# Sparse attention with both key groups in one iteration and zero-padded operands, in a two-block model on one core

## Chip, core and metric

The kernel runs on one core of one Trainium2 chip. The metric is the device time of one execution in microseconds; the median of three runs before the change is 2191.86 us (2190.61 to 2194.94). A profile of one execution gives the instructions of each engine: PE (TensorE), DVE (VectorE), ACT (ScalarE), POOL (GpSimd) and the DMA queues. The program itself is put in order at build time: every engine gets a fixed list of instructions, and semaphores make one engine wait for another.

## What is computed

256 tokens of width 1024 pass through a first block (a mixer of three branches, then a mixture of experts with 16,384 small experts) and a second block (feed-forward layers, a convolution mixer, differential attention). The change lies in two branches of the mixer.

The **stick-breaking branch** has 8 heads of 64: scores z, then weights exp(log sigmoid(z) + the sum of log sigmoid(-z) over the keys between), times the values. In short:

```python
log_1m = where(before, log_sigmoid(-z), 0.0)
after = cumsum(log_1m, reverse=True) - log_1m
a = where(before, exp(log_sigmoid(z) + after), 0.0); out = a @ v
```

The **sparse branch** (NSA) has 8 heads of 64 in two groups; the four heads of a group share keys and values. A query attends in three ways, each with its own softmax and its own gate: to 15 compressed keys (each made of 32 neighbouring tokens by a product with a [2048, 64] matrix), to selected blocks of 64 keys, and to a window. At 256 tokens there are four blocks and four are selected, and the window is 256 long, so these two read all earlier keys:

```python
s = q @ k.T * scale - slope * dist
p = softmax(where(valid, s, -1e30)); o = g0*p_c@v_c + g1*p_s@v_s + g2*p_w@v_w
```

## The kernel before, in words

All weights come as a stream of units [128, 1024] of float32. `Stream.next` (L252) issues a unit's DMA on SP's queue, ScalarE makes a rounded copy `whi` (L268) and VectorE the rest `wlo` (L269). `proj_T` (L75) multiplies a unit by the 256 tokens with three matmuls per tile of 128 rows (`mm3`, L68 to L73): 24 records of 256 columns a unit. Four raw and three finished units can be held at a time.

`mixer` (from L1056) is the phase of the change. `proj2` makes two such projections into one PSUM bank (tag pp, two banks) and evacuates it. The other banks are five of tag bk for everything between and one of tag ob for a branch's output. The phase runs HGRN2 (a linear recurrence, L1115 to L1219), stick breaking (L1221 to L1263), NSA (L1266 to L1381), then 24 units of projections for the merge gates (L1384 to L1386), the gated sum of the three branches (L1396 on) and the output projection. The order on each engine is not that of the text: at build time a scheduler that works with estimated costs takes, for each engine, the earliest instruction of the text that is ready. So where an attention chain waits for another engine, TensorE's list has projection matmuls of later steps (pp) in between.

**Stick breaking**, one head at a time (L1238). Two heads lie in one tile of 128 rows, so that a head's queries and keys are 64 rows. A head's scores of 256 + 128 columns (L1245, L1246), its causal mask added by a bfloat16 product with the identity (L1247, L1248), three exponential-type steps of ScalarE over 384 columns (L1250 to L1252), one step of VectorE, products with a triangle for the running sums (L1254 to L1256), one more exponential (L1258), and the product with the values, 64 output rows (L1260, L1261).

**Compression** (L1286 to L1310). `xa` holds for each of the 32 places of a block the tokens of 16 blocks for both groups, 64 rows a group, zero where row and column belong to different groups. For keys and then for values 32 matmuls run over it, with 64 columns standing and 64 moving (L1303).

**Attention of NSA** (L1329 to L1381): for four pairs p, two groups gg and two tiles of queries qt, 16 iterations:

```python
q = nq[ks, p, qt * 128 : qt * 128 + 128]              # 64 rows
mm(sc[...], q, nk[ks, a, :kl], start=True, stop=False)  # a = 0, 1
mm(sc[...], ident_b, bias[:, h, 256 - kl :], start=False, stop=True)
mm(sc2[:, :16], q, kcT[ks, :], start=True, stop=False)
```

with kl 128 or 256. Maxima (L1346, L1347), exponentials with sums (L1352, L1354), reciprocal, gates and scaling (L1356 to L1360), transposes by TensorE (L1363, L1367), copies out of PSUM (L1371, L1372), products with the values (L1378) and with the compressed values (L1380). The output of a pair goes through `put` (L1106 to L1108). A float32 matmul appears as two records in the trace, a transpose or a bfloat16 matmul as one.

## Time and profile before

| what | value |
|---|---|
| median of the runs | 2191.86 us |
| span of the profiled execution | 2191.6 us |
| TensorE busy | 99% of the span |
| VectorE, ScalarE, POOL busy | 68%, 53%, 1% |
| granted TensorE clock, mean | 0.997 |
| read from memory | 367.38 MB |

The span runs from the first to the last instruction of the profiled execution; that execution's time beyond the span is not in the profile, and the median of the other runs stands 0.3 us above it. A busy time of TensorE adds up modelled ends of matmuls that overlap; the distance from one start to the next is in the timeline.

### The profile page before, as it was taken

The numbers are of one execution on the slowest core, as the hardware profiler recorded it, in microseconds if no ns is written. First come the engines' busy times: TensorE is split into PE (matmuls) and PEld (weight loads), VectorE is DVE, ScalarE is ACT, GpSimd is POOL, SyncE is SP. The second block draws the span as 40 slices with busy tenths as digits, with TensorE's granted clock in tenths as the row PEclk, the third lists the DMA queues.
The fourth block names the chain that finished last, engine by engine and source line by source line (L and its number), as shares of the span: only waits on it lengthen the run. The fifth ranks groups of instructions, "written<-read, shape, count | busy, mean of one in ns | idle before, by whom it ended". The sixth has DMA issues, their size and how long they took to land.

```text
span 2191.6 us, 37898 instructions
## 1 busy us (share of the span) xinstructions
PE 2161.8 (99%) x14823; PEld 1979.5 (90%) x14823; DVE 1480.1 (68%) x2705; ACT 1152.1 (53%) x2088; POOL 26.7 (1%) x27
## 2 busy tenths in 40 slices
PE   8999999999999999999999999999999999999998
PEld 7978898999999998888888999999999999878998
DVE  5865658799888895556557655776557555677554
ACT  5544354554577775554446544545446444466443
POOL 0000000000000000000000000000000000100000
PEclk9999999999999999999999999999999999999999
DMA  7334245555544445656555755556655654534652
GB/s 232 104 110 126 78 143 176 164 183 184 183 136 135 135 135 184 193 195 213 195 193 174 253 187 183 188 168 209 192 183 174 209 185 154 183 106 144 203 183 97
DMA packets 103010, 370.89 MB, mean 169 GB/s; under 512 B 12208, under 2 KB 12976, under 8 KB 102704
## 3 DMA queue, kind: packets, MB, share of 16 engines
q1 hardware_dynamic: 102688, 367.69, 52.1%
q8 instruction: 117, 1.92, 0.4%
q0 software_dynamic: 144, 0.79, 0.1%
q14 instruction: 61, 0.50, 0.1%
HBM read 367.38 MB, written 1.05 MB: 168 GB/s over the span
## 4 chain that ended last, share of the span: by engine, by line
PE 93%; DVE 3%; ACT 1%; issue 1%; DMA 0%; SPq 0%; DVEq 0%; ACTq 0%
PE gu L72 9%; PE gu L73 9%; PE gu L71 9%; PE hp L71 6%; PE hp L72 6%; PE hp L73 6%; PE pacc L72 5%; PE pacc L71 5%; PE pacc L73 5%; PE acc L72 5%; PE acc L71 5%; PE acc L73 5%; PE pp L71 3%; PE pp L73 3%; PE pp L72 3%; PE gp L885 3%
## 5 line engine op out<-in xcount | busy, mean ns | idle before, releaser
L268 ACT ACTIVATE whi<-raw 128x1024 fp32r<-128x1024 f32 x670 | 704.0, 1058 | 791.0 <-PE gu L72 214.5
L269 DVE TENSOR_TENSOR wlo<-raw,whi 128x1024 fp32r<-128x1024 f32 x670 | 819.4, 1225 | 355.9 <-ACT whi L268 352.9
L71 PE MATMUL gu<-hT,whi 128*128 128x256 f32 x1568 | 444.7, 284 | 0.4 <-ACT sg L438 0.4
L73 PE MATMUL gu<-hT,wlo 128*128 128x256 f32 x1568 | 444.3, 283 | 0.3 <-DVE wlo L269 0.3
L72 PE MATMUL gu<-hT,whi 128*128 128x256 f32 x1568 | 444.3, 283 | 0.0
L71 PEld LDWEIGHTS gu<-hT,whi 128*128 128x128 f32 x1568 | 300.1, 191 | 3.5 <-ACT sg L438 0.6
L72 PEld LDWEIGHTS gu<-hT,whi 128*128 128x128 f32 x1568 | 300.4, 192 | 2.7
L73 PEld LDWEIGHTS gu<-hT,wlo 128*128 128x128 f32 x1568 | 300.4, 192 | 0.5 <-DVE wlo L269 0.5
L71 PE MATMUL hp<-hT,whi 128*128 128x256 f32 x1024 | 294.8, 288 | 1.0 <-ACT Ga L850 1.0
L73 PE MATMUL hp<-hT,wlo 128*128 128x256 f32 x1024 | 289.7, 283 | 0.0
L72 PE MATMUL hp<-hT,whi 128*128 128x256 f32 x1024 | 289.6, 283 | 0.0
L71 PEld LDWEIGHTS hp<-hT,whi 128*128 128x128 f32 x1024 | 196.2, 192 | 1.4 <-ACT Ga L850 1.2
L72 PEld LDWEIGHTS hp<-hT,whi 128*128 128x128 f32 x1024 | 196.3, 192 | 0.2
L71 PE MATMUL pacc<-whi,pa 128*128 128x512 f32 x504 | 196.1, 389 | 0.0
L72 PE MATMUL pacc<-wlo,pa 128*128 128x512 f32 x504 | 196.1, 389 | 0.0
L73 PEld LDWEIGHTS hp<-hT,wlo 128*128 128x128 f32 x1024 | 196.1, 191 | 0.0
L73 PE MATMUL pacc<-whi,pa 128*128 128x512 f32 x504 | 196.1, 389 | 0.0
L72 PE MATMUL acc<-wlo,a 128*128 128x512 f32 x352 | 138.9, 395 | 0.0
L73 PE MATMUL acc<-whi,a 128*128 128x512 f32 x352 | 138.2, 393 | 0.0
L71 PE MATMUL acc<-whi,a 128*128 128x512 f32 x352 | 136.8, 391 | 0.0
L452 DVE TENSOR_TENSOR sg<-gu,rbc 128x256 f32<-128x256 f32 x80 | 33.9, 423 | 132.3 <-PE gu L73 132.3
L73 PE MATMUL pp<-hT,wlo 128*128 128x256 f32 x416 | 119.7, 288 | 0.0
(431 smaller groups left out, 3555.0 us busy)
## 6 DMA issues: line engine op xcount, KB each, us to landing
raw<-w_peer_dram SPq DMA_DIRECT2D x264, 512.0 KB, 3.4
raw<-w_ffn_dram SPq DMA_DIRECT2D x264, 512.0 KB, 4.1
raw<-w_mix_dram SPq DMA_DIRECT2D x83, 512.0 KB, 3.7
raw<-w_conv_dram SPq DMA_DIRECT2D x32, 512.0 KB, 4.3
raw<-w_qo_dram SPq DMA_DIRECT2D x16, 512.0 KB, 4.0
g<-g_norm_dram SPq DMA_DIRECT2D x12, 512.0 KB, 3.8
raw<-w_k_dram SPq DMA_DIRECT2D x8, 512.0 KB, 3.4
raw<-w_v_dram SPq DMA_DIRECT2D x8, 512.0 KB, 4.7
```

The costliest lines, as they stand in the source:

```text
L71: mm(out, l[0], r[0], start=start, stop=False)
L72: mm(out, l[0], r[1], start=False, stop=False)
L73: self.last_mm = mm(out, l[1], r[0], start=False, stop=stop)
L268: c.nc.scalar.activation(hi, raw, AF.Copy)
L269: c.last_lo = c.nc.vector.tensor_tensor(lo, raw, hi, op=ALU.subtract)
L452: V.tensor_tensor(sg, gu[:, 0, :], c.rbc, op=ALU.mult)
L885: nc.tensor.matmul(gp[:, m, :], r, cg, start=True, stop=True)
```

## The change

- Stick breaking: `sbq` has a second copy of each pair's space, zeroed by POOL, in which each head's queries fill their own 64 rows; a head's scores then use all 128 rows of `sbk`. Two heads run side by side; two of the three exponential steps take both at once; the products with the values alternate between the two heads. The work tiles come from a pool of their own, opened after HGRN2's is closed and closed after NSA.
- Compression: the rows of `xa` are now 64 dimensions of the even and 64 of the odd places, so that 16 steps do instead of 32; keys and values alternate, into the two halves of one bank.
- NSA: `nk`, `kcT` and `vc` have room for both groups, zero where the other group's rows are. One iteration handles the heads p and p + 4: one query tile of 128 rows against both groups' keys, 512 columns to a matmul. The validity factor moves into the gates. The products with the values alternate between the groups' halves of the output.

Comments and docstrings are left out of the new file. The rest of the difference:

```diff
@@ -1012,5 +1012,6 @@
     P = {"w_mix": u, "g_mix": bc(i["norm_mix"][0])}
-    wc = np.stack([i["nsa_w_cmp_k"][0], i["nsa_w_cmp_v"][0]]).reshape(2, 32, 64, 64).transpose(2, 0, 1, 3)
-    P["w_cmp"] = np.concatenate([wc, wc])
-    P["pe"] = np.ascontiguousarray(np.concatenate([i["nsa_cmp_pe"][0].T] * 2))
+    wc = np.stack([i["nsa_w_cmp_k"][0], i["nsa_w_cmp_v"][0]]).reshape(2, 16, 2, 64, 64)
+    P["w_cmp"] = np.ascontiguousarray(wc.transpose(2, 3, 0, 1, 4).reshape(128, 2, 16, 64))
+    pe = i["nsa_cmp_pe"][0].reshape(16, 2, 64).transpose(2, 1, 0)
+    P["pe"] = np.ascontiguousarray(np.concatenate([pe, pe]))
     P["hnorm"] = np.ascontiguousarray(i["hgrn_norm"][0].reshape(4, 128).T)
@@ -1221,3 +1222,5 @@
-        sbq = pool.tile([128, 4, T], F32, name="sbq")
+        sbq = pool.tile([128, 4, 2, T], F32, name="sbq")
+        G.memset(sbq, 0.0)
         sbk = pool.tile([128, 4, T], F32, name="sbk")
@@ -1230,5 +1233,9 @@
         V.tensor_copy(sbmb, sbm)
+        def sbq_evac(p, b):
+            for hh in range(2):
+                hs = slice(hh * 64, hh * 64 + 64)
+                A.activation(sbq[hs, p : p + 2, hh, :], b[hs].rearrange("p (a t) -> p a t", a=2), AF.Copy, scale=0.125)
         for p in range(2):
-            proj2(sbq[:, 2 * p : 2 * p + 2, :].rearrange("p a t -> p (a t)"),
-                  lambda d, b: A.activation(d, b, AF.Copy, scale=0.125))
+            proj2(2 * p, sbq_evac)
         for p in range(2):
@@ -1237,28 +1244,34 @@
         proj_mv(512, lambda nt, b: A.activation(sbv[:, nt, :], b, AF.Copy))
-        for h in range(8):
...
-            A.activation(sp, z[:, :384], AF.Abs)
+        work = ExitStack()
+        sbw = work.enter_context(tc.tile_pool(name="sbw", bufs=1))
+        for p in range(4):
+            ob = bank("ob")
+            zs, aw = [], []
+            sp = sbw.tile([128, 2, 384], F32, name=f"sbsp{p}", tag="sbsp", bufs=2)
+            for hh in range(2):
+                z = bank()
+                mm(z[:, 0:256], sbk[:, p, 0:128], sbq[:, p, hh, :], start=True, stop=False)
+                mm(z[:, 256:384], sbk[:, p, 128:256], sbq[:, p, hh, 128:256], start=False, stop=False)
+                mm(z[:, 0:128], ident_b, sbmb, start=False, stop=False)
+                mm(z[:, 256:384], ident_b, sbmb, start=False, stop=True)
+                A.activation(sp[:, hh, :], z[:, :384], AF.Abs)
+                zs.append(z)
             A.activation(sp, sp, AF.Exp, scale=-1.0)
             A.activation(sp, sp, AF.Ln, bias=1.0)
-            V.scalar_tensor_tensor(sp, z[:, :384], 0.0, sp, op0=ALU.max, op1=ALU.add)
...
-                put("sb", p, ob[:, :256])
+            for hh, z in enumerate(zs):
+                s_ = sp[:, hh, :]
+                V.scalar_tensor_tensor(s_, z[:, :384], 0.0, s_, op0=ALU.max, op1=ALU.add)
+                mm(z[:, 0:256], tri[:, 0, :], s_[:, 0:256], start=False, stop=False, skip_group_check=True)
+                mm(z[:, 128:256], tri[:, 1, :], s_[:, 256:384], start=False, stop=True, skip_group_check=True)
+                mm(z[:, 256:384], tri[:, 0, :], s_[:, 256:384], start=False, stop=True, skip_group_check=True)
+                a = sbw.tile([128, 384], F32, name=f"sba{p}{hh}", tag="sba", bufs=3)
+                A.activation(a, z[:, :384], AF.Exp)
+                aw.append(a)
+            for st in range(2):
+                for hh, a in enumerate(aw):
+                    vs = slice(p * 128 + hh * 64, p * 128 + hh * 64 + 64)
+                    ks = slice(hh * 64, hh * 64 + 64)
+                    mm(ob[ks, st * 128 : 256], sbv[:, st, vs], a[:, st * 256 : st * 128 + 256], start=st == 0, stop=st == 1)
+            put("sb", p, ob[:, :256])
@@ -1266,4 +1279,5 @@
         with tc.tile_pool(name="ns", bufs=1) as npool:
-            wc = npool.tile([128, 2, 32, 64], F32, name="wc")
-            pe = npool.tile([128, 32], F32, name="pe")
+            wc = npool.tile([128, 2, 16, 64], F32, name="wc")
+            pe = npool.tile([128, 2, 16], F32, name="pe")
             nc.sync.dma_start(wc, P["w_cmp"])
@@ -1271,3 +1285,3 @@
-            xa = npool.tile([128, 2, 32, 2, 32], F32, name="xa")
+            xa = npool.tile([128, 2, 16, 2, 32], F32, name="xa")
             G.memset(xa, 0.0)
@@ -1279,7 +1293,18 @@
             nc.sync.dma_start(valid, P["cvalid"])
-            bias = npool.tile([128, 8, 256], BF16, name="abias")
-            biasc = npool.tile([128, 8, 2, 16], BF16, name="abiasc")
+            bias = npool.tile([128, 4, 2, 256], BF16, name="abias")
+            biasc = npool.tile([128, 4, 2, 2, 16], BF16, name="abiasc")
             for h in range(8):
-                V.tensor_scalar(bias[:, h, :], dist, 2.0 ** -(h + 1), None, op0=ALU.mult)
-                V.tensor_scalar(biasc[:, h], dc, 2.0 ** -(h + 1), None, op0=ALU.mult)
+                V.tensor_scalar(bias[:, h % 4, h // 4, :], dist, 2.0 ** -(h + 1), None, op0=ALU.mult)
+                V.tensor_scalar(biasc[:, h % 4, :, h // 4, :], dc, 2.0 ** -(h + 1), None, op0=ALU.mult)
+            nk = npool.tile([128, 2, 2, T], F32, name="nk")
+            G.memset(nk, 0.0)
+            kcT = npool.tile([128, 2, 16], F32, name="kcT")
+            V.memset(kcT, 0.0)
+            vc = npool.tile([128, 128], F32, name="vc")
+            V.memset(vc, 0.0)
+            ecs = [npool.tile([128, 2, 64], F32, name=f"nec{i}") for i in range(2)]
+            for e in ecs:
+                V.memset(e, 0.0)
@@ -1289,7 +1314,8 @@
                         gs = slice(gg * 64, gg * 64 + 64)
-                        src = b[gs, a * 256 : a * 256 + 256].rearrange("p (c l) -> p l c", l=16)
-                        for r in range(2):
-                            ls = slice(r * 16, r * 16 + 16)
-                            V.tensor_tensor(xa[gs, a, ls, gg, 0:15], src[:, :, r : r + 15],
-                                            pe[gs, ls, None].broadcast_to((64, 16, 15)), op=ALU.add)
+                        src = b[gs, a * 256 : a * 256 + 256].rearrange("p (c m e) -> p e m c", m=8, e=2)
+                        for par in range(2):
+                            for r in range(2):
+                                ls = slice(r * 8, r * 8 + 8)
+                                V.tensor_tensor(xa[par * 64 : par * 64 + 64, a, ls, gg, 0:15], src[:, par, :, r : r + 15],
+                                                pe[gs, par, ls, None].broadcast_to((64, 8, 15)), op=ALU.add)
@@ -1297,18 +1323,18 @@
             kc = npool.tile([16, 128], F32, name="kc")
-            kcT = npool.tile([128, 16], F32, name="kcT")
...
-                    A.activation(kcT, bt[:, :16], AF.Copy)
+            cb = bank()
+            for l in range(16):
+                for a in range(2):
+                    mm(cb[a * 64 : a * 64 + 64, :64], xa[:, a, l].rearrange("p g c -> p (g c)"), wc[:, a, l, :],
+                       start=l == 0, stop=l == 15)
+            for gg in range(2):
+                gs = slice(gg * 64, gg * 64 + 64)
+                A.activation(kc[:, gs], cb[gg * 32 : gg * 32 + 16, :64], AF.Copy)
+                A.activation(vc[gg * 64 : gg * 64 + 16, gs], cb[64 + gg * 32 : 80 + gg * 32, :64], AF.Copy)
+            bt = bank()
+            nc.tensor.transpose(bt[:, :16], kc, c.ident[:16, :16])
+            for gg in range(2):
+                gs = slice(gg * 64, gg * 64 + 64)
+                A.activation(kcT[gs, gg, :], bt[gs, :16], AF.Copy)
             nq = npool.tile([128, 4, T], F32, name="nq")
-            nk = npool.tile([128, 2, T], F32, name="nk")
             nv = npool.tile([128, 2, 256], F32, name="nv")
@@ -1318,3 +1344,9 @@
                       lambda d, b: A.activation(d, b, AF.Copy, scale=0.125))
-            proj2(nk.rearrange("p a t -> p (a t)"), lambda d, b: V.tensor_copy(d, b))
+            def nk_evac(d, b):
+                for gg in range(2):
+                    gs = slice(gg * 64, gg * 64 + 64)
+                    V.tensor_copy(nk[gs, :, gg, :], b[gs].rearrange("p (a t) -> p a t", a=2))
+            proj2(None, nk_evac)
             gf = gts.rearrange("p a h r -> p a (h r)")
@@ -1328,56 +1360,73 @@
             A.activation(gf, gf, AF.Exp, scale=-1.0)
+            for qt in range(2):
+                V.tensor_scalar(gts[:, qt, :, 0], gts[:, qt, :, 0], valid[:, qt : qt + 1], None, op0=ALU.mult)
+            nk4 = nk.rearrange("p a g t -> p (a g) t")
             for p in range(4):
                 ob = bank("ob")
-                for gg in range(2):
...
-                            V.tensor_scalar(e[:, a, :kl], e[:, a, :kl], sm[:, a + 1 : a + 2], None, op0=ALU.mult)
+                for qt in range(2):
+                    kl = 128 * (qt + 1)
+                    u = f"{p}{qt}"
+                    q = nq[:, p, qt * 128 : qt * 128 + 128]
+                    per = 2 // (qt + 1)
+                    sc = [bank().rearrange("p (k t) -> p k t", t=kl) for _ in range(2 // per)]
+                    sc2 = bank()
+                    for i, b in enumerate(sc):
+                        mm(b, q, nk4[:, 2 * per * i : 2 * per * (i + 1), :kl], start=True, stop=False)
+                        bb = bias[:, p, :, 256 - kl :]
+                        if per == 2:
+                            bb = bb[:, None].broadcast_to((128, 2, 2, kl))
+                            b = b.rearrange("p (a g) t -> p a g t", a=2)
+                        mm(b, ident_b, bb, start=False, stop=True)
+                    mm(sc2[:, :32], q, kcT.rearrange("p g c -> p (g c)"), start=True, stop=False)
+                    mm(sc2[:, :32], ident_b, biasc[:, p, qt].rearrange("p g c -> p (g c)"), start=False, stop=True)
+                    mx = npool.tile([128, 6], F32, name=f"nmx{u}", tag="nmx", bufs=3)
+                    V.tensor_reduce(mx[:, 0:2], sc2[:, :32].rearrange("p (g c) -> p g c", g=2), axis=AX.X, op=ALU.max,
+                                    negate=True)
+                    for i, b in enumerate(sc):
+                        V.tensor_reduce(mx[:, 2 + 2 * per * i : 2 + 2 * per * (i + 1)], b, axis=AX.X, op=ALU.max, negate=True)
+                    e = npool.tile([128, 4, 256], F32, name=f"ne{u}", tag="ne", bufs=2)
+                    ec = ecs[qt]
+                    sm = npool.tile([128, 6], F32, name=f"nsm{u}", tag="nsm", bufs=3)
+                    for gg in range(2):
+                        A.activation(ec[:, gg, :16], sc2[:, gg * 16 : gg * 16 + 16], AF.Exp, bias=mx[:, gg : gg + 1],
+                                     accum_out=sm[:, gg : gg + 1])
+                    for k in range(4):
+                        last_exp = A.activation(e[:, k, :kl], sc[k // (2 * per)][:, k % (2 * per), :], AF.Exp,
+                                                bias=mx[:, k + 2 : k + 3], accum_out=sm[:, k + 2 : k + 3])
+                    V.reciprocal(sm, sm)
+                    V.tensor_tensor(sm.rearrange("p (r g) -> p r g", g=2), sm.rearrange("p (r g) -> p r g", g=2),
+                                    gts[:, qt].rearrange("p (g q) r -> p q r g", g=2)[:, p], op=ALU.mult)
+                    V.tensor_tensor(ec[:, :, :16], ec[:, :, :16], sm[:, 0:2, None].broadcast_to((128, 2, 16)), op=ALU.mult)
+                    pt2 = sc2[:, 128:256]
+                    nc.tensor.transpose(pt2, ec.rearrange("p g c -> p (g c)"), c.ident)
+                    pTc = npool.tile([128, 128], F32, name=f"npTc{u}", tag="npTc", bufs=2)
+                    pT = npool.tile([128, 8, 128], F32, name=f"npT{u}", tag="npT", bufs=2)
+                    for i in range(2 // per):
+                        ks = slice(2 * per * i, 2 * per * (i + 1))
+                        V.tensor_tensor(e[:, ks, :kl], e[:, ks, :kl],
+                                        sm[:, 2 + 2 * per * i : 2 + 2 * per * (i + 1), None].broadcast_to((128, 2 * per, kl)),
+                                        op=ALU.mult)
                         pt = bank()
-                        pt2 = bank()
...
-                        mm(o, vc[:, ks], pTc, start=False, stop=True)
+                        for k in range(4):
+                            nc.tensor.transpose(pt[:, k * 128 : k * 128 + 128],
+                                                e[:, 2 * per * i + k // (qt + 1), k % (qt + 1) * 128 : k % (qt + 1) * 128 + 128],
+                                                c.ident)
+                        if i == 0:
+                            V.tensor_copy(pTc, pt2)
+                        V.tensor_copy(pT[:, 4 * i : 4 * i + 4, :], pt.rearrange("p (k t) -> p k t", k=4))
+                    o = ob[:, qt * 128 : qt * 128 + 128]
+                    mm(o, vc, pTc, start=True, stop=False, skip_group_check=True)
+                    for a in range(2):
+                        for st in range(qt + 1):
+                            for gg in range(2):
+                                mm(o[gg * 64 : gg * 64 + 64], nv[:, st, a * 128 + gg * 64 : a * 128 + gg * 64 + 64],
+                                   pT[:, (a * 2 + gg) * (qt + 1) + st, :], start=False, stop=a == 1 and st == qt,
+                                   skip_group_check=True)
                 put("nsa", p, ob[:, :256])
+        work.close()

```

## Rows read from the trace of the kernel before

**Rows 1.** The page: busy time by engine, and the chain that ended last
```profile
PE 2161.8 (99%) x14823; PEld 1979.5 (90%) x14823; DVE 1480.1 (68%) x2705; ACT 1152.1 (53%) x2088; POOL 26.7 (1%) x27
...
PE 93%; DVE 3%; ACT 1%; issue 1%; DMA 0%; SPq 0%; DVEq 0%; ACTq 0%
```

**Rows 2.** Waits of TensorE, whole run: line, releaser, us, times, longest
```profile
PE pt L148 <- DVE xs L170: 9.8, 2, 9.2
...
PE bk L1363 <- DVE nec L1358: 0.4, 2, 0.2
```

**Rows 3.** Windows: us, PE, PEld, DVE, ACT, POOL (records), clock, DMA, GB/s
```profile
129.50:157.00 27.50, 27.50 (x163) 20.85 (x162) 11.69 (x32) 19.05 (x41) 3.51 (x1) 1.00 0.34 123
...
160.40:169.00 8.60, 8.60 (x135) 8.29 (x134) 2.87 (x6) 0.61 (x3) 0.00 (x0) 1.00 0.17 65
169.00:190.70 21.70, 21.70 (x178) 21.62 (x176) 9.55 (x9) 10.29 (x14) 0.00 (x0) 1.00 0.52 149
190.70:297.80 107.10, 106.71 (x736) 85.68 (x734) 65.29 (x172) 40.81 (x122) 0.00 (x0) 1.00 0.29 89
297.80:319.30 21.50, 21.50 (x180) 21.50 (x180) 12.24 (x12) 10.55 (x10) 0.00 (x0) 1.00 0.68 196
```

**Rows 4.** Timeline of TensorE at 154.6: start, us, line, operands, form, count
```profile
154.57 0.59 PE L1254 MATMUL bk<-sbsp,tri 128*128 128x256 f32 x2
155.00 0.38 PE L1255 MATMUL bk<-sbsp,tri 128*128 128x128 f32 x2
155.22 0.39 PE L1256 MATMUL bk<-sbsp,tri 128*128 128x128 f32 x2
```

**Rows 5.** The same timeline at 147.3, masks
```profile
147.30 0.22 PE L1247 MATMUL bk<-sbmb,mident 128*128 128x128 bf16 x1
147.36 0.22 PE L1248 MATMUL bk<-sbmb,mident 128*128 128x128 bf16 x1
```

**Rows 6.** The same timeline, 234.2 to 237.2, scores of one head
```profile
234.23 0.70 PE L1341 MATMUL bk<-nk,nq 64*128 64x256 f32 x2
234.85 0.28 PE L1342 MATMUL bk<-abias,mident 128*128 128x256 bf16 x1
...
236.85 0.39 PE L1343 MATMUL bk<-kcT,nq 64*128 64x16 f32 x2
...
237.21 0.36 PE L71 MATMUL pp<-hT,whi 128*128 128x256 f32 x1
```

**Rows 7.** The same timeline at 148.2, one visit to 64 output columns
```profile
148.18 0.28 PE L73 MATMUL pp<-hT,wlo 128*128 128x256 f32 x1
148.39 0.65 PE L1260 MATMUL ob<-sba,sbv 128*64 128x256 f32 x2
148.87 0.38 PE L1261 MATMUL ob<-sba,sbv 128*64 128x128 f32 x2
149.18 0.70 PE L1254 MATMUL bk<-sbsp,tri 128*128 128x256 f32 x2
149.72 0.38 PE L1255 MATMUL bk<-sbsp,tri 128*128 128x128 f32 x2
```

**Rows 8.** The same timeline at 217.2, values of one head
```profile
217.18 1.09 PE L1378 MATMUL ob<-npT,nv 128*64 128x128 f32 x8
218.19 0.43 PE L1380 MATMUL ob<-npTc,vc 16*64 16x128 f32 x2
```

**Rows 9.** The same timeline at 160.4, compression
```profile
160.40 3.94 PE L1303 MATMUL bk<-wc,xa 128*64 128x64 f32 x64
```

**Rows 10.** Timeline of POOL at 133.8
```profile
133.82 3.51 POOL L1273 MEMSET xa<- 128x4096 f32 x1 [118.72 <-DVE ohg L1108]
```

**Rows 11.** Instructions of xa: ns min/median/max, first and last start
```profile
L1293 DVE TENSOR_TENSOR xa<-pp,pe x8: 390/402/411, 159.1 to 161.7; 64x240 f32<-64x240 f32 x8
```

**Rows 12.** Groups by form, 190.7 to 297.8: busy us, mean ns, idle before
```profile
L1347 DVE TENSOR_REDUCE nmx<-bk 128x2 f32<-128x512 f32 x8 | 5.5, 687 | 7.9 <-PE bk L1342 7.9
...
L1354 ACT ACTIVATE ne<-bk,nmx 128x256 f32<-128x256 f32 x16 | 7.5, 469 | 14.2 <-DVE nmx L1347 8.3 <-DVE nmx L1346 5.9
```

More of the change, by code (lines that the diff above doesn't have):

```diff
@@ L1237, in mixer @@
         proj_mv(512, lambda nt, b: A.activation(sbv[:, nt, :], b, AF.Copy))
-        for h in range(8):
-            p, off = h // 2, (h % 2) * 64
-            ks = slice(off, off + 64)
-            if h % 2 == 0:
-                ob = bank("ob")
-            z = bank()
-            mm(z[:, 0:256], sbk[ks, p, 0:128], sbq[ks, p, :], start=True, stop=False)
-            mm(z[:, 256:384], sbk[ks, p, 128:256], sbq[ks, p, 128:256], start=False, stop=False)
-            mm(z[:, 0:128], ident_b, sbmb, start=False, stop=False)
-            mm(z[:, 256:384], ident_b, sbmb, start=False, stop=True)
-            sp = pool.tile([128, 384], F32, name=f"sbsp{h}", tag="sbsp", bufs=2)
-            A.activation(sp, z[:, :384], AF.Abs)
+        work = ExitStack()
@@ L1251, in mixer @@
             A.activation(sp, sp, AF.Exp, scale=-1.0)
             A.activation(sp, sp, AF.Ln, bias=1.0)
-            V.scalar_tensor_tensor(sp, z[:, :384], 0.0, sp, op0=ALU.max, op1=ALU.add)
-            mm(z[:, 0:256], tri[:, 0, :], sp[:, 0:256], start=False, stop=False, skip_group_check=True)
-            mm(z[:, 128:256], tri[:, 1, :], sp[:, 256:384], start=False, stop=True, skip_group_check=True)
-            mm(z[:, 256:384], tri[:, 0, :], sp[:, 256:384], start=False, stop=True, skip_group_check=True)
@@ L1257, in mixer @@
-            a = pool.tile([128, 384], F32, name=f"sba{h}", tag="sba", bufs=2)
-            A.activation(a, z[:, :384], AF.Exp)
-            vs = slice(h * 64, h * 64 + 64)
-            mm(ob[ks, 0:256], sbv[:, 0, vs], a[:, 0:256], start=True, stop=False)
-            mm(ob[ks, 128:256], sbv[:, 1, vs], a[:, 256:384], start=False, stop=True)
-            if h % 2 == 1:
-                put("sb", p, ob[:, :256])
+            for hh, z in enumerate(zs):
[7 more added lines that the diff above has]
+                aw.append(a)
@@ L1299, in mixer @@
-            vc = npool.tile([16, 128], F32, name="vc")
-            for a, dst in enumerate((kc, vc)):
-                b = bank()
-                for l in range(32):
-                    mm(b[:64, :64], xa[:, a, l].rearrange("p g c -> p (g c)"), wc[:, a, l, :],
-                       start=l == 0, stop=l == 31)
-                for gg in range(2):
-                    A.activation(dst[:, gg * 64 : gg * 64 + 64], b[gg * 32 : gg * 32 + 16, :64], AF.Copy)
-                if a == 0:
-                    bt = bank()
-                    nc.tensor.transpose(bt[:, :16], kc, c.ident[:16, :16])
-                    A.activation(kcT, bt[:, :16], AF.Copy)
+            cb = bank()
```

46 lines of the change are left out of this document (removed).

## Prediction, made before the changed kernel was run

> **What bounds the kernel now.** The page comes first: TensorE is busy 99% of a span of 2191.6 us and holds 93% of the chain that ended last [rows 1]. Busy alone proves little, since a record (one matmul instruction of the trace) lasts longer than the step to the next one, so I read the waits next. Over the whole run the longest thing that a matmul waits for is 9.8 us at the very start, and in the sparse branch it is 0.4 us in two places [rows 2]. The engine's queue is therefore full, and what counts is the step from one start to the next. The stretches give it: 297.8 to 319.3 holds nothing but 180 records of projections in 21.5 us, or 0.119 us each, at full clock [rows 3]. That is the price of the filler (projection matmuls that the scheduler puts between the dependent ones).
>
> With it the three stretches that the change touches can be split. In all three an f32 matmul is two records, a transpose or a bf16 matmul one. Stick breaking: 163 records, of which 8 heads x 16 = 128 are its own; 27.5 - 35 x 0.119 = 23.3 us. Compression: 135 records, 129 its own; 8.6 - 6 x 0.119 = 7.9 us. Sparse attention: 736 records, of which 8 heads x (18 + 24 for the two tiles) = 336 its own; 107.1 - 400 x 0.119 = 59.3 us [rows 3]. Together 90.5 us of TensorE time, and this is what the change can cut.
>
> **Prices of a record.** With all 128 rows, f32: 256 columns 0.43 / 2 = 0.215, 128 columns 0.22 / 2 = 0.11 [rows 4]. 512 columns have no row; as 128 to 256 doubles, I take 0.43. bf16, 128 columns: 0.06, so 512 columns 0.22 [rows 5]. With 64 rows, 256 columns cost 0.62 / 2 = 0.31 [rows 6]: 0.1 more than the same columns with 128. A visit to the form with 64 output columns costs extra at four places: 0.21 for 0.12, 0.48 for 0.43, 0.31 for 0.22, 0.54 for 0.43 [rows 7], sum 0.34 us. Inside a visit, 128 moving columns step by about 0.11 (8 records and the way out in 1.01 us [rows 8]); 64 moving columns step by 3.94 / 64 = 0.06 [rows 9].
>
> **Sparse attention, after.** Heads p and p + 4 run in one iteration, 8 in place of 16. Scores: 128 rows, padded with zeros, 512 columns at once: 0.86 for the matmul and 0.22 for the bias; one such for tile 0, two for tile 1: 4 x 1.08 + 4 x 2.16 = 13.0. Compressed scores, 32 columns: at most the 64-row pair with its bias, 0.36 [rows 6], at least two 0.11 loads and a 0.06 bias, 0.28; I take 0.3, x 8 = 2.4. Transposes: 48 stay, 16 become 8, at 0.11: 6.2. Values of the compressed keys: 16 records of 128 rows at 0.11: 1.8. Values: still 96 records of 64 output columns, but now the two column halves alternate, which no row shows. Ends: 0.11 each, if a half waits for the other [rows 8], and 0.06, the shortest step of this form [rows 9]. A record follows one of its own half half the time (the two records of an f32 matmul); I give those 0.11 and the others 0.06, so 0.084: 96 x 0.084 = 8.1 (ends 10.6 and 5.6). Visits 8 x 0.34 = 2.7. Sum 34.2 us, saving 25.1 (22.6 to 27.6).
>
> **Stick breaking, after.** The score matmuls get 128 rows: 16 x 0.215 + 16 x 0.11 = 5.2; masks 16 x 0.06 = 0.9; triangles 16 x 0.215 + 32 x 0.11 = 7.0; values 5.2 in turn, 2.6 overlapped, 3.9 by the same half rule; 4 visits 1.4. Sum 18.4, saving 4.9 (3.6 to 6.2).
>
> **Compression, after.** 64 records in place of 128, halves alternating; at 0.06 the weight load already fills the step, so I take no overlap: 3.8, with one visit and the small transpose 4.3; saving 3.6 (5.4 if the halves overlap).
>
> **What is hidden.** The zeroing on POOL (2048, 2048 and 1024 columns by 3.51 us for 4096 [rows 10], 4.4 us) stands in front of evacuations: xa's zeroing starts at 133.8 and its evacuation at 159.1 [rows 10, 11], and for the queries' POOL is idle 118.7 us before; uncovered, it would delay them by its own length. The compression's evacuation becomes 16 half-size VectorE instructions at 0.4 us or less for 8 [rows 11], up to 3.2 us more; nq's projections (most of the 178 records of 169 to 190.7) can run meanwhile, and uncovered it costs those 3.2. The new work area of stick breaking may lie where HGRN's tiles were, whose release came at 133.8 by POOL's row [rows 10], 4.3 us after the stretch began; projections cover that too, else up to 4 us. Two more scaled copies of queries on ScalarE, one more copy of keys and a few fills of VectorE, under 3 us in all, lie on engines busy 19 of 27.5 and 65 of 107 us [rows 3]. The weight of the compression is 1 MB less on SP's queue, at a DMA share of 0.17 to 0.34 [rows 3], so I cost it at nothing.
>
> Does the chain of an iteration stay hidden? Tile 1: scores 2.5, second maximum 0.69, six exponentials at most 0.47 each, 2.8 [rows 12], four short VectorE steps and the gate at an assumed 0.2 each, 0.8, two scalings and two copies of 512 columns like the maximum's, 2.8, a short copy 0.3, values 1.5: 11.4 us. Eight of them end to end are 91 us. The TensorE work from 190.7 to the end of the filler at 319.3 would be 128.6 - 25.1 = 103.5 us, so even without overlap there is work to put in. What is late next is still TensorE.
>
> **Sum.** 25.1 + 4.9 + 3.6 = 33.6 us off the profiled 2191.6 gives 2158.0. The median of the runs, 2191.86 (2190.61 to 2194.94), is 0.3 above the profile, which changes nothing. About 0.2%, 4.4 us, is what a measurement of this kernel can tell from no change.
>
> **A rule weighed.** The 64-row records step by 0.31, the 128-row ones by 0.215 [rows 4, 6]; padding saves the difference. The Trainium skill's page "TensorE: Matmul & The Clock Gate", section "Why this matters for your kernels", says that a matmul with few rows takes as long as one with 128 and that the gain lies in running several row tiles at once: by it padding buys nothing and gives a chance away. The row disagrees for this kernel, whose 64-row records stand alone; by the row the sum is the 2158 above, by the page the 0.1 would stay on the padded records, the third rival's 2163.
>
> **Rivals.**
> **No overlap:** the column halves do not overlap at all: 22.6 + 3.6 + 3.6 = 29.8, so 2162. For it: every row of this form steps by its columns. Against: nothing was alternated there.
> **Full overlap:** 27.6 + 6.2 + 5.4 = 39.2, so 2152. For it: the array changes its form at a visit, at a cost [rows 7], as one that is divided would. The Trainium skill's "TensorEngine Tiling (Array Packing)", section "Key Properties", says that different tiles can load and multiply in parallel; no run so far shows it.
> **Exposed loads:** the padded records keep an exposed load of 0.1 each, because it does not come from the 64 rows: 24 score records and 32 of stick breaking, 5 us less, so 2163. Against: rows 4 are hidden loads of just that form.
> **Slower:** the filler fails. One iteration's 11.4 us chain then shows, less its own 34.2 / 8 = 4.3 of TensorE work: 8 x 7.1 = 57 us of stops in place of 33.6 us saved, 2215. ScalarE's queue could do it: weights' copies wait behind six exponentials, and five banks hold one tile-1 iteration only. It turns the sign once 60% of the chain is bare. Against: two waits of 0.4 us in all today [rows 2]. A weaker form, a part of this, ends between 2165 and 2190.
>
> **How the numbers follow.** Half overlap 0.38 (2158), none 0.30 (2162), full 0.20 (2152), exposed loads 0.03, partial stops 0.07 (0.02 of it within 0.2%), filler failing 0.02. The range from 2149 to 2168 takes the first four with their unknowns (two to three us each way) and leaves out the stops and the tails. Faster 0.96, same 0.02, slower 0.02.
>
> **What would show it.** In the new trace the score records step by 0.43, with no 64-row form left in this branch; the values step by 0.11, 0.084 or 0.06; the three stretches, filler taken off at 0.119, sum to 57 us (60 without overlap, 52 with); no matmul waits over 1 us between 130 and 300. It is wrong if the filler between iterations runs out before the eighth, or if the stages behind the merge move.

## The result, and the profile after

The changed kernel takes 2159.62 us (median of 4 runs, 2158.14 to 2162.99), the kernel before in the same session 2193.1: ratio 0.985, 95% interval [0.984, 0.986]. Run a second time, on another occasion, it took 2162.79 (2157.68 to 2164.66; ratio 0.986 [0.984, 0.987]).

The profiled execution has a span of 2160.9 us and a time of 2162.99, so 2.1 us lie around a span. The page's busy line shows no new bound:

```profile
PE 2126.5 (98%) x14647; PEld 1954.8 (90%) x14651; DVE 1471.9 (68%) x2652; ACT 1151.1 (53%) x2083; POOL 28.6 (1%) x29
```

The waits of TensorE's matmuls over the whole run begin with the first row (us in total, times, longest); the second row is the answer for 131 to 330 us, and the only one there. The third is from the waits of its weight loads (PEld) in the same time:

```profile
PE pt L148 <- DVE xs L170: 10.4, 2, 9.8
...
PE bk L1376 <- issue: 0.2, 1, 0.2
...
PEld bk L1265 <- DVE sbsp L1264: 0.8, 3, 0.4
```

So the filler held in all three stretches, but for short waits ahead of stick breaking's triangles, 0.8 us in three places. The windows of the stretches (columns as in [rows 3]): stick breaking, compression, sparse attention, and one of pure filler:

```profile
131.40:157.60 26.20, 26.20 (x178) 21.35 (x177) 12.54 (x39) 18.65 (x34) 2.70 (x2) 1.00 0.33 108
157.60:165.30 7.70, 7.70 (x106) 7.10 (x105) 6.02 (x17) 2.41 (x7) 0.00 (x0) 1.00 0.21 59
...
184.50:250.40 65.90, 65.36 (x502) 53.36 (x504) 48.65 (x99) 35.58 (x118) 0.00 (x0) 1.00 0.33 99
...
286.60:321.10 34.50, 34.50 (x290) 34.50 (x289) 27.62 (x33) 17.54 (x17) 0.00 (x0) 1.00 0.59 184
```

Filler is again 34.5 / 290 = 0.119 us a record. Own records now: 128 in stick breaking, 65 in compression, 228 in sparse attention, of which 4 biases are missing from the trace. With the filler taken off: 26.2 - 50 x 0.119 = 20.2; 7.7 - 41 x 0.119 = 2.8; 65.9 - 278 x 0.119 = 32.8. Together 55.8 in place of 90.5 us, 34.7 less.

A second measure needs no filler price. VectorE makes the low parts of the weights in a fixed order; the 25th of them starts ahead of the changed code and the 65th behind it. In the timeline of VectorE, after:

```profile
98.14 1.21 DVE L269 TENSOR_TENSOR wlo<-raw,whi 128x1024 fp32r<-128x1024 f32 x1
...
284.88 1.23 DVE L269 TENSOR_TENSOR wlo<-raw,whi 128x1024 fp32r<-128x1024 f32 x1 [1.65 <-ACT whi L268]
```

and before:

```profile
95.97 1.23 DVE L269 TENSOR_TENSOR wlo<-raw,whi 128x1024 fp32r<-128x1024 f32 x1
...
317.62 1.23 DVE L269 TENSOR_TENSOR wlo<-raw,whi 128x1024 fp32r<-128x1024 f32 x1 [1.65 <-ACT whi L268]
```

The distance is 221.65 before and 186.74 after: 34.9 us less (186.69 in the second profile of the changed kernel, so it repeats within 0.1). Outside it, executions differ though no edit reaches there: over the 13 profiles of this study the 25th part starts at 95.3 to 98.9 us, and from the 65th to the last take 1852.7 to 1859.0. Whole times of one kernel spread by as much, about 5 us, so the experiments are judged by this distance, called **the stretch** below, with the whole time beside it.

What the new forms cost. The timeline of TensorE in one iteration of sparse attention:

```profile
214.78 1.02 PE L1376 MATMUL bk<-nk,nq 128*128 128x512 f32 x2
215.74 0.66 PE L1425 MATMUL ob<-npT,nv 128*64 128x128 f32 x8
216.33 0.39 PE L1381 MATMUL bk<-abias,mident 128*128 128x512 bf16 x1
...
216.72 0.36 PE L72 MATMUL pp<-hT,whi 128*128 128x256 f32 x1
216.93 0.28 PE L73 MATMUL pp<-hT,wlo 128*128 128x256 f32 x1
...
217.14 0.66 PE L1425 MATMUL ob<-npT,nv 128*64 128x128 f32 x8
217.72 0.39 PE L71 MATMUL pp<-hT,whi 128*128 128x256 f32 x1
```

Eight value records with the way in and out take 216.33 - 215.74 = 0.59 us, 1.01 in [rows 8]: the starts of two halves are 7 ns apart, the next two follow 0.109 later. A pair costs what one record cost. The rows show three more things: the values of one tile come in two visits (215.74 and 217.14), the second score record in front of a visit takes 0.52 in place of 0.43 (214.78 to 215.74, two in 0.96), and the filler record behind own work takes 0.21 (216.72 to 216.93) in place of 0.12. Compression:

```profile
162.28 2.08 PE L1327 MATMUL bk<-wc,xa 128*64 128x64 f32 x62
164.29 0.39 PE L72 MATMUL pp<-hT,whi 128*128 128x256 f32 x1
```

62 records in 2.01 us, 0.032 each, where 64 took 3.94 [rows 9]. Stick breaking is different:

```profile
141.49 1.04 PE L1275 MATMUL ob<-sba,sbv 128*64 128x256 f32 x8
142.46 0.70 PE L1265 MATMUL bk<-sbsp,tri 128*128 128x256 f32 x2
143.00 0.38 PE L1266 MATMUL bk<-sbsp,tri 128*128 128x128 f32 x2
...
144.41 0.65 PE L1275 MATMUL ob<-sba,sbv 128*64 128x256 f32 x2
144.99 0.70 PE L1254 MATMUL bk<-sbq,sbk 128*128 128x256 f32 x2
145.62 0.86 PE L1275 MATMUL ob<-sba,sbv 128*64 128x256 f32 x6
146.41 0.38 PE L1255 MATMUL bk<-sbq,sbk 128*128 128x128 f32 x1
```

The second pair of heads needs two visits, 0.58 and 0.79 us, with a score matmul between: the first head's two records ran alone before the second head's weights were there. The 32 value records take 5.1 us in all, over seven visits.

### The profile page after: what moved, and what is told of

Its sections match the earlier page's. It is cut to its first block, busy times and chain, and to the rows that moved or that the text cites. A ratio compares the mean times of both kernels' runs of the same rounds, so it can differ in the third digit from the quotient of the medians.

```text
span 2160.9 us, 37488 instructions
## 1 busy us (share of the span) xinstructions
PE 2126.5 (98%) x14647; PEld 1954.8 (90%) x14651; DVE 1471.9 (68%) x2652; ACT 1151.1 (53%) x2083; POOL 28.6 (1%) x29
## 3 DMA queue, kind: packets, MB, share of 16 engines
HBM read 366.33 MB, written 1.05 MB: 170 GB/s over the span
## 5 line engine op out<-in xcount | busy, mean ns | idle before, releaser
L71 PE MATMUL pp<-hT,whi 128*128 128x256 f32 x416 | 118.9, 286 | 0.0
```

Source lines behind the costliest of these rows:

```text
L71: mm(out, l[0], r[0], start=start, stop=False)
```

## Experiments

**One part at a time** (three kernels, each the kernel before with one part of the change):

```diff
 sb_only
+        sbq = pool.tile([128, 4, 2, T], F32, name="sbq")
...
 cmp_only
+            for l in range(16):
+                for a in range(2):
+                    mm(cb[a * 64 : a * 64 + 64, :64], xa[:, a, l].rearrange("p g c -> p (g c)"), wc[:, a, l, :],
...
 nsa_only
+            nk = npool.tile([128, 2, 2, T], F32, name="nk")
...
```

> The kernel before with the new stick breaking alone. Theory (the time is TensorE's record time, and what a stage loses comes off the end one for one, whatever the other stages do): the stretch from the first score to the last value product, filler taken off at 0.119 us a record, falls from 23.3 to about 20, the whole by 3 to 4 us, 0.998 of before. Rival (the order of the lists decides: filler moves, and a stage alone gives its gain back in the next stage's stops): nothing, or a loss, with a new wait of TensorE of over 1 us between 130 and 330 us.

> The kernel before with the compression in 16 steps alone. Theory: 64 records fewer and the two halves of the bank overlapping: the stretch's own time falls from 7.9 to about 3 us, the whole by 4.5 to 5 us, 0.998 of before; successive records of different halves start under 0.01 us apart. Rival (order decides): under 2 us, because the evacuation has 16 instructions in place of 8 and TensorE has to wait for it.

> The kernel before with the new sparse attention alone (compression in 32 steps, stick breaking head by head). Theory: its own TensorE time falls from 59.3 to about 33, the whole by 25 to 27 us, 0.988 of before; the three parts alone then add up to the 33 of the full change within 3 us. Rival (order decides): the parts alone sum to under 25 or over 40.

| kernel | stretch, us | against before | median, us | ratio [95%] |
|---|---|---|---|---|
| stick breaking alone | 218.13 | -3.5 | 2192.09 | 0.9996 [0.9986, 1.0005] |
| compression alone | 216.35 | -5.3 | 2189.40 | 0.9978 [0.9969, 0.9988] |
| sparse attention alone | 195.33 | -26.3 | 2166.09 | 0.9881 [0.9864, 0.9897] |
| all three (the changed kernel) | 186.74 | -34.9 | 2159.62 | 0.985 [0.984, 0.986] |

The parts add up: 3.5 + 5.3 + 26.3 = 35.1 against 34.9, so none leans on another. Stick breaking's 3.5 us can't be told from nothing by the whole time; only the trace shows it.

**Halves in turn.** The changed kernel, with the loops so ordered that one half's matmuls are issued before the other's:

```diff
-            for st in range(2):
-                for hh, a in enumerate(aw):
+            for hh, a in enumerate(aw):
+                for st in range(2):
...
-            for l in range(16):
-                for a in range(2):
+            for a in range(2):
+                for l in range(16):
...
-                    for a in range(2):
-                        for st in range(qt + 1):
-                            for gg in range(2):
+                    for gg in range(2):
+                        for a in range(2):
+                            for st in range(qt + 1):
```

> The changed kernel with the column halves one after the other: all value products of one head (or group) before those of the other, all keys' steps of the compression before the values'. Same matmuls, another order. Overlap theory (a record of the other half starts at once, one of its own half waits): value records of the sparse attention step by 0.11 in place of a pair in 0.11, so about 4 us more there, 1.5 us more in the compression, about 0.5 in stick breaking: 6 us above the changed kernel, 2165. Half theory of the prediction: 2.4 + 0 + 1.2, 3.6 us. No-overlap rival: no difference, 2160.

Stretch 190.38, 3.6 us longer than the changed kernel's; median 2164.32, ratio 0.9865 [0.9849, 0.9882]. By place, from the same marks: stick breaking about 0.4, compression 1.3, sparse attention 2.0. The total is that of the half rule, but its parts were to be 1.2, nothing and 2.4. The timeline of TensorE says why, first the compression, with the row of VectorE's writing of its operands `xa` (16 instructions, first and last start), then the values of a tile 1:

```profile
158.82 2.08 PE L1327 MATMUL bk<-wc,xa 128*64 128x64 f32 x32
160.83 0.38 PE L73 MATMUL pp<-hT,wlo 128*128 128x256 f32 x1
161.14 1.15 PE L1327 MATMUL bk<-wc,xa 128*64 128x64 f32 x16
...
L1319 DVE TENSOR_TENSOR xa<-pp,pe x16: 265/277/286, 156.6 to 160.6; 64x120 f32<-64x120 f32 x16
...
234.21 0.65 PE L1425 MATMUL ob<-npT,nv 128*64 128x128 f32 x4
234.80 0.39 PE L1381 MATMUL bk<-abias,mident 128*128 128x512 bf16 x1
235.12 1.10 PE L1425 MATMUL ob<-npT,nv 128*64 128x128 f32 x12
236.15 0.41 PE L1382 MATMUL bk<-kcT,nq 128*128 128x32 f32 x2
```

In the compression, with 16 matmuls of one half in a row, every record steps by 0.058: truly in turn, and twice the 0.029 of the alternating order. In the values, 4 records take 0.59 (no overlap), but the 12 at 235.12 take 1.03: four pairs and four single records, 8 x 0.11 and the way in and out. A half does not wait for its place in the order of issue: its record starts beside the other half's, though two matmuls of that half were issued ahead of it (its partner is the first of the two). How far this reaches the compression can't tell: the values' operands were still being written until after 160.6, while the keys' matmuls ran from 158.82, and a filler record stood between the halves. So this edit undid all of the overlap only in the compression, and half of it in a tile 1; the rule of the prediction (a half waits when the record before is its own) is not what they show.

**The heads of stick breaking together.** The changed kernel; the value products of a pair are issued second head first, so that none starts before both heads' weights are there:

```diff
+            prev = None
             for st in range(2):
-                for hh, a in enumerate(aw):
+                for hh in (1, 0):
...
+                    with tc.issue_after(prev.ins) if prev else ExitStack():
+                        prev = mm(ob[ks, st * 128 : 256], sbv[:, st, vs], aw[hh][:, st * 256 : st * 128 + 256],
+                                  start=st == 0, stop=st == 1)
```

> The changed kernel, but in stick breaking the value products of a pair of heads are issued only when the second head's weights are there: the second head's first, then the first head's, the four of a pair in one visit. Theory 1 (the halves overlap whenever both heads' weights are ready, and the 5.1 us that the 32 records take in the changed kernel are heads that are ready one after the other, in seven visits): 4 visits x (0.05 + 2 x 0.215 + 2 x 0.11 + 0.1) = 3.2 us, so the stretch shortens by 1.9 us against the changed kernel. Theory 2 (256 columns of two halves do not overlap, whatever the order): 4 x (0.15 + 4 x 0.215 + 4 x 0.11) = 5.8 us, so the stretch is 0.5 us longer or the same. Whole time: 2158 by the first, 2161 by the second, both within the spread of the changed kernel's runs, so the records decide.

Stretch 184.22, 2.5 us shorter than the changed kernel's; median 2158.59, ratio 0.985 [0.984, 0.986]. The timeline of one pair:

```profile
139.64 0.87 PE L1277 MATMUL ob<-sba,sbv 128*64 128x256 f32 x8
140.44 0.70 PE L1265 MATMUL bk<-sbsp,tri 128*128 128x256 f32 x2
```

0.80 us a pair, 3.2 in all, as theory 1 had it. That is 1.9 of the 2.5; another 0.4 is triangle records (7.2 us in place of 7.7), fewer of which stand next to a visit, while the scores take the same (5.85 and 5.84). What stick breaking's values lacked was a ready partner.

**Row halves in place of padding.** The padded operands make one 128-row matmul of two 64-row ones. The other way is to run the two 64-row ones at once. The changed kernel with unpadded keys or queries (first diff sparse attention, second stick breaking, the third kernel has both), and the changed kernel itself beside them:

```diff
+                    for g, b in enumerate(sc):
+                        gs = slice(g * 64, g * 64 + 64)
+                        mm(b, q[gs], nk[gs, :, :kl], start=True, stop=False)
...
+            for st in range(2):
+                for hh, z in enumerate(zs):
+                    ks = slice(hh * 64, hh * 64 + 64)
+                    mm(z[:, st * 256 : st * 128 + 256], sbk[ks, p, st * 128 : st * 128 + 128], sbq[ks, p, st * 128 : 256],
...
```

> The changed kernel as it is, for a yardstick on the chip of the next three: 2159.6 us within 2, ratio to the kernel before 0.985.

> The changed kernel, but with unpadded keys in the sparse branch: each group's scores are a matmul of 64 rows, the two groups' matmuls next to each other, in the two row halves, each into a bank of its own. In the changed kernel 24 score records of 512 columns step by 0.43 us, 10.3 us in all. Theory 1 (row halves run beside each other, as the column halves of the compression do): 16 records of 256 and 16 of 512 columns, half of them free, about 5.2 us, plus eight visits to another form at 0.34, 2.7: some 2.4 us less than the changed kernel, 2157. Theory 2 (a 64-row record does not hide its load and does not overlap): 16 x 0.31 + 16 x 0.53 = 13.4 us plus the visits 2.7: some 6 us more, 2166. Theory 3 (they overlap in part, the load stays open): between, within 1 us of the changed kernel. The scores' step between the two row halves tells them apart: some ns, 0.5 us, or between.

> The changed kernel, but with unpadded queries in stick breaking: the two heads' scores are matmuls of 64 rows, next to each other, in the two row halves, each into its head's bank. In the changed kernel 16 records of 256 columns and 16 of 128 take 5.9 us there. Theory 1 (overlap): 2.6 us plus four visits at 0.34, 1.4: 1.9 us less, 2157.7. Theory 2 (no overlap, open loads of 0.1): 16 x 0.31 + 16 x 0.21 = 8.3 us plus 1.4: 3.8 us more, 2163.4. Theory 3 (in part): within 1 us of the changed kernel.

> Both of the last two edits together, no padding left in either branch. Theory 1: the sum of the two gains, 4 us less than the changed kernel, 2155.5. Theory 2: the sum of the two losses, 10 us more, 2169. Theory 3: within 2 us of it.

| kernel | stretch, us | against the changed one | median, us | ratio [95%] |
|---|---|---|---|---|
| changed kernel again | 186.69 | -0.1 | 2162.79 | 0.986 [0.984, 0.987] |
| row halves, sparse attention | 184.98 | -1.8 | 2160.58 | 0.985 [0.984, 0.986] |
| row halves, stick breaking | 186.57 | -0.2 | 2160.20 | 0.986 [0.984, 0.987] |
| both | 184.75 | -2.0 | 2157.85 | 0.984 [0.983, 0.985] |

The changed kernel itself came out 3.2 us above its first median, more than the 2 that were expected; its stretch did not move.

TensorE's timeline of the kernel with row halves in sparse attention, scores (L1373) of the first tile 0, of a tile 1, and of another tile 0:

```profile
185.07 0.70 PE L1373 MATMUL bk<-nk,nq 64*128 64x256 f32 x4
185.70 0.39 PE L1375 MATMUL bk<-abias,mident 128*128 128x256 bf16 x2
...
206.38 1.13 PE L1373 MATMUL bk<-nk,nq 64*128 64x512 f32 x4
207.44 0.33 PE L1419 MATMUL ob<-npT,nv 128*64 128x128 f32 x2
...
199.06 0.70 PE L1373 MATMUL bk<-nk,nq 64*128 64x256 f32 x2
199.68 0.66 PE L1419 MATMUL ob<-npT,nv 128*64 128x128 f32 x8
200.27 0.70 PE L1373 MATMUL bk<-nk,nq 64*128 64x256 f32 x2
200.90 0.39 PE L1375 MATMUL bk<-abias,mident 128*128 128x256 bf16 x2
```

Next to each other, four records take 0.63 us, as long as the two of a single matmul [rows 6]. With 512 columns four take 1.06, or 0.53 a pair. Where the values came between (199.06 to 200.90, in three of the four tiles 0), two records take 0.62 and nothing overlaps. Theory 1 holds for every pair that stays together, theory 2 for every pair that is torn apart.

In stick breaking one of the four pairs of heads was torn, and the score records still fell from 5.9 to 4.5 us. But the stretch kept 0.2 of that. TensorE now waited for VectorE ahead of the triangles, in two places:

```profile
PE bk L1261 <- DVE sbsp L1260: 1.0, 2, 0.6
```

What the scores saved went into waiting for the chain that makes the triangles' operand, and into the masks behind the 64-row form (1.2 us in place of 0.8).

**Row halves for tile 1 alone, values in one visit.** The changed kernel:

```diff
+                        for g in (1, 0):
+                            gs = slice(g * 64, g * 64 + 64)
+                            with tc.issue_after(prev.ins) if prev else ExitStack():
+                                prev = mm(sc[g], q[gs], nk[gs, :, g, :], start=True, stop=False)
...
-                    for a in range(2):
+                    for a in (1, 0):
```

> The changed kernel, but tile 1 of the sparse branch takes its scores in the two row halves (64 rows of the padded keys for each group, each group in its own bank, the second group's first), tile 0 keeps the padded 128-row form, and the eight value products of a tile 1 are issued in one visit. Theory 1 (a pair of 512-column records in the two row halves takes 0.53 us, as in the fully paired places of the run with both row tiles): tile 1's scores take 4 x 2 x 0.53 = 4.2 us in place of 4 x 4 x 0.43 = 6.9, 2.7 us less; four visits fewer at 0.15, 0.6 less: the stretch is 3.3 us shorter than in the changed kernel, 2157. Theory 2 (what the row halves save comes back at the bias, the transposes and the values next to them): 1 us shorter at most, 2159.

Stretch 184.78, 2.0 us shorter; median 2159.60, ratio 0.985 [0.984, 0.986]. Between the two theories, for a reason that neither had: two of the four pairs of scores were torn by the values, as TensorE's timeline shows.

```profile
205.74 1.12 PE L1384 MATMUL bk<-nk,nq 64*128 64x512 f32 x2
206.79 0.66 PE L1433 MATMUL ob<-npT,nv 128*64 128x128 f32 x8
207.38 1.12 PE L1384 MATMUL bk<-nk,nq 64*128 64x512 f32 x2
208.43 0.60 PE L1386 MATMUL bk<-abias,mident 128*128 128x512 bf16 x2
```

A torn pair takes 2 x 1.05 us, a whole one 1.06 to 1.08, so the two torn ones cost 2.1 us together, more than the 1.3 that is missing. Some 0.3 of the difference is the scores of tile 0, which no longer stand in front of the values; the rest I have not placed.

**All of it together.** The last edit, the paired values, and stick breaking's scores in row halves, the third and fourth pair held back behind the values of the first and second:

```diff
+            prev = lastv[p - 2] if p > 1 else None
+            for st in range(2):
+                for hh in (1, 0):
...
+                    with tc.issue_after(prev.ins) if prev else ExitStack():
+                        prev = mm(zs[hh][:, st * 256 : st * 128 + 256], sbk[ks, p, st * 128 : st * 128 + 128],
+                                  sbq[ks, p, hh, st * 128 : 256], start=st == 0, stop=False)
```

> The last two edits together, and stick breaking's scores in the two row halves as well, each pair kept together by issuing the third and fourth pairs' scores behind the value products of two pairs before. Theory 1: 3.3 + 1.9 + 4 x (4 x 0.215 + 4 x 0.11 + 0.06 - 0.85) = 2.0, 7.2 us off the changed kernel's stretches, 2153 to 2155. Theory 2 (the tighter order makes TensorE wait, which the filler does not cover): waits of over 0.5 us at the value products or the scores, and less than 3 us gained.

Stretch 181.66, 5.1 us shorter than the changed kernel's, where theory 1 had 7.2. The last edit and the paired values had given 2.0 and 2.5, so the row halves of stick breaking added 0.6 in place of 2.0. In the trace three of the four pairs of heads have their scores in 0.85 us (eight records), and a wait of the kind that theory 2 named stands ahead of the triangles, as with row halves in stick breaking alone:

```profile
131.07 0.92 PE L1258 MATMUL bk<-sbq,sbk 64*128 64x256 f32 x8
131.92 0.23 PE L1261 MATMUL bk<-sbmb,mident 128*128 128x128 bf16 x1
```

```profile
PE bk L1269 <- DVE sbsp L1268: 1.1, 2, 0.8
```

Yet the median is 2159.86 (2158.60 to 2163.41), ratio 0.985 [0.984, 0.987], no different from the changed kernel's. 0.8 us are given back by the 101st low part; the remaining 4 lie inside the spread of the start and the tail. Whether an execution of this kernel gives more back later than one of the changed kernel is open: one profile of it can't say. No version is shown to beat the changed kernel in whole time; the lowest median is that of row halves in both branches, 2157.85 (2155.61 to 2158.99), with an interval that overlaps the changed kernel's.

## Why the prediction was right

It said 2158.0 (2149 to 2168); the runs say 2159.62 and 2162.79. Its sum was 33.6 us off the stretches; they lost 34.9. What carried it is right: TensorE's own records in three stretches are the cost, and the filler covers nearly all the rest. That the total came within 1.3 us is in part luck: the terms missed by 1.2, 1.4 and 1.7, and not all the same way. The terms:

- **Sparse attention**, 25.1: measured 26.3. Padding did its work: the 24 score records of 512 columns step by 0.43, or 0.52 where a visit to the values follows (214.78), so the rival "exposed loads" falls here. The values were mis-sized in both directions. Forecast 8.1 for the records by the half rule and 2.7 for eight visits, 10.8 together; measured 7.1 to 7.3 with all visits, at 0.055 a record and 0.15 a visit, though there are twelve visits, since a tile 1 brings its values in two. The forecast's 0.34 a visit counts two records more, the one ahead (0.52 for 0.43) and the one behind (0.21 for 0.12); with them the twelve come near 0.34 each as well, and the values, by this estimate, to some 9.3. What ate most of that gain is a term the sum did not have: filler next to own work, 0.21 in place of 0.12 (216.72), which makes the 275 filler steps of this window 0.133 on average, about 4 us. The 404 filler steps of the kernel before were 0.133 too, and what they took above 0.119, 5.4 us, stands in the 59.3 but not in the 34.2.
- **Stick breaking**, 4.9: measured 3.5, just under its lower end of 3.6. The step that failed is the price of scores and triangles, 0.215 for each record of 256 columns, the clean step of [rows 4]. The first record behind another form takes more (142.46 to 143.00, two records in 0.54), and so do two first triangles behind filler (139.06 and 150.17, 0.32 each), whose weight load waited for VectorE (the PEld row above). The 16 triangle records of 256 columns took 3.98 us and the 16 score records 3.98, each 0.5 above the sum; the 51 filler records took 1.0 more than 0.119 each, which the sum left out here too. The values came out near the forecast (5.1 against 3.9 + 1.4) but not by overlap: seven visits, mostly one head alone.
- **Compression**, 3.6: measured 5.3. The failed step is "at 0.06 the weight load already fills the step, so I take no overlap". Loads of the two halves run beside each other as the matmuls do; the pair steps by 0.058, where one record did before.
- **What is hidden**: nothing of the zeroing, the 16 evacuations or the longer chain shows as a wait of a matmul above 0.2 us between 131 and 330; stick breaking's chain shows in three waits of weight loads, 0.8 us in all. The compression did wait for its evacuations (two records at 159.9, the rest from 162.28), with filler between, as argued.
- **The rivals.** "No overlap" and "filler fails" fall by the rows above. "Full overlap" has the right mechanism and still the wrong time, since it took the other prices from the same list; 2152 would have needed the paired heads, one visit a tile and filler at its clean price. The half rule, which carried the forecast, is wrong as a mechanism: its total came out, by luck, because full overlap in two places, little in a third and the dearer filler happen to average to it.
- **The rule weighed.** Padding pays, as forecast, but not for the reason given. The prediction read [rows 6], two records in 0.62, as 0.31 for each 64-row record, 0.1 above the 128-row price. Stick breaking before shows what that 0.1 is:

```profile
129.50 0.70 PE L1245 MATMUL bk<-sbq,sbk 64*128 64x256 f32 x2
130.04 0.38 PE L1246 MATMUL bk<-sbq,sbk 64*128 64x128 f32 x2
130.35 0.23 PE L1247 MATMUL bk<-sbmb,mident 128*128 128x128 bf16 x1
```

These four records take 0.54 and 0.31, 0.85 in all, where [rows 4] has 0.43 and 0.22 with 128 rows. The 0.2 more is there once for four records, as it is once for two in [rows 6]: 0.1 goes to the first of a visit to the 64-row form and 0.1 to the last, and a record between them costs the same with 64 rows as with 128. What padding saved is the visits. The sum did not suffer, since it took the kernel before from measured stretches and the padded records from 128-row rows. By the Trainium skill, "TensorE: Matmul & The Clock Gate", section "Why this matters for your kernels", the gain of few rows lies in running row tiles at once; here a pair at 0.53 did what two padded records of 0.43 do, 0.86, where the pair stayed together. The 2 us that this gave in the stretch are what padding leaves. That different tiles load and multiply in parallel (the Trainium skill, "TensorEngine Tiling (Array Packing)", section "Key Properties") is now shown for both directions, 7 ns between the starts.
- **Slips.** 96 x 0.06 is 5.8, not 5.6; the 0.1 on 24 + 32 records is 5.6, not 5; the 9.8 us of waiting at the start are two waits, the longer of 9.2 [rows 2]. None moves the forecast.
- **Profile and time.** The prediction set the span of 2191.6 against the median and saw 0.3 between them. A time lies 2.1 us above its span here, so the profiled execution of before was no median one; the later medians of the same kernel are 2192.9 to 2193.6.

## What to carry to other kernels

Two f32 matmuls that use different halves of the array, columns or rows, cost one if both are ready and stand close together in the queue; so before counting on it, look at when the second operand is ready and what the scheduler puts between, and bind the pair by issuing the later one first. What a pair saves is kept only where the engine has other work until the next operand is ready: with row halves in stick breaking, 1.4 us less of scores left 0.2. Padding to 128 rows is the form that can't be torn apart, at a cost of some 0.3 us a pair against row halves that stay together. An edit worth 2 to 5 us of 2160 is read from the distance between two fixed points of the trace on either side of it, since the whole time moves by as much from run to run.

## What the runs showed of the hardware

- **The halves run as two streams.** In the kernel with halves in turn, the second head's first value record started 0.18 us after the first head's, and ahead of the first head's second matmul, which had been issued before it. In sparse attention the same held with two matmuls of one half issued ahead of the other half's first; how far it goes is not shown.
- **A pair of 64-row records costs what one costs.** In the last kernel eight records of two heads took 0.85 (131.07 to 131.92), and in the kernel before four records of one head took 0.85 (129.50 to 130.35). A visit to the 64-row form costs 0.2 more than the same columns with 128 rows, once.
- **The clock drops in most executions**, outside the change: at 1920 to 1970 us in 11 of the 13 profiles, and near 1160 in four. Windows of 10 us (clock third from the end), after and then before:

```profile
1930.00:1940.00 10.00, 9.63 (x36) 6.60 (x36) 5.96 (x20) 4.77 (x22) 0.00 (x0) 0.66 0.31 101
```

```profile
1960.00:1970.00 10.00, 9.63 (x32) 6.30 (x30) 5.05 (x16) 3.70 (x15) 0.00 (x0) 0.54 0.28 87
```

0.54 is almost all at 1.2 GHz. TensorE was busy 9.16 of the 10 us just ahead of either; with row halves in stick breaking it was busy 9.16 there too, and the clock stayed at 1.00. The profile of sparse attention alone has no drop anywhere, and the shortest time of all from the 65th low part to the last, 1852.7 us. So it is likely one source of the spread of whole times.
